# Rotation by a lane shuffle, three gate tiles moved ahead, and latent-attention scores for two heads at a time, in a two-layer encoder trunk

## The chip, the cores and the metric

The kernel runs on one core of one Trainium2 chip. The metric is the device time of one execution in microseconds (us), as the median of several executions. The engines are named as in the profile: PE (TensorE, matrix products), DVE (VectorE), ACT (ScalarE), POOL (GpSimd) and SP (SyncE, which issues the loads). Each engine works through its own list of instructions in a fixed order, and semaphores tie the lists together: an instruction whose input isn't ready holds up all that stands behind it on its engine.

## The reference

256 tokens of width 2048 pass through two layers; all numbers are fp32. What bears on the change is the first half of a layer:

```python
z = rmsnorm(x, g_mix[i]) @ w_in[i]
dq, dk, dv, cq, ckv, kr, ga, gb = split(z)      # 1024, 1024, 1024, 512, 256, 64, 2048, 2048 columns
# A: 8 heads, two softmax maps each (64 wide): weights = probs0 - lam * probs1; od = weights @ dv
qf = rmsnorm(cq) @ w_q_up                       # 8 heads of 128 + 64: q_nope, q_rope
kvf = rmsnorm(ckv) @ w_kv_up                    # 8 heads of 128 + 128: k_nope, v
k_rope = apply_rope(kr)                         # 64 wide, one for all heads
# B: scores = (q_nope @ k_nope + apply_rope(q_rope) @ k_rope) * scale; om = softmax(scores) @ v
m = sigmoid(ga) * (od_normed @ w_branch_diff) + sigmoid(gb) * (om @ w_branch_mla)
x = x + m @ w_out
```

`apply_rope` takes the halves x1 and x2 of the 64 columns and gives x1\*c - x2\*s and x2\*c + x1\*s: column d is combined with column d ± 32. Behind this come the SwiGLU feed-forward part and the gated embedding of the layer, which the change doesn't touch.

## The kernel before, in words

**Layout.** Tokens lie along the free axis (256), features along the 128 partitions. An activation tile is kept as two halves, `[hi | lo]`, 512 columns (`split`, L247: ACT writes hi, DVE the difference). A weight piece of 128x1024 is loaded by SP and split in the same way by ACT (`whi`, L187) and DVE (`wlo`, L187 too, recorded under L75): `piece`, L173. A product (`product`, L220; `pair`, L231, for two output tiles of a narrower weight) then runs for each 128x128 weight tile one matmul of 512 columns (hi times `[hi | lo]`, L212) and one of 256 columns (lo times hi, L216). The text calls these two a pair of matmuls. `joined` (L240) adds the two halves of the result: an ACT copy, `join`, and a DVE addition, `a`.

**Order of the first half of a layer.** The values of the differential attention come first, then the latents, then the loop over eight differential heads (`pipelined`, L650). For a head, `scores` (L398) makes two 128x256x2 maps by twelve 64-row matmuls (L406, maps in turn), `exps` (L409) takes the maxima (DVE, L412) and exponentials (ACT, L415), two blocks b per map; the weights are turned by PE (`turned`, L419 to L426: four transposes at L424, one ACT copy `wt`, L426), and `diff_out` (L626) multiplies them with the values (PE, L632), copies the result out (ACT, `fa`, L635) and sums its squares (ACT, L637). Between these steps, the generator `beside` (L573) hands out other products to fill PE: queries and keys of later heads, `keys_up`, the shared key through `narrow` and `rotated`, then `queries_up` for n = 8, 0, 2, 10 (8 and 10 are the rotated parts), `settle` (L639, transposes at L647), and last n = 4 and 6. Then come the latent values, and a second `pipelined` loop over eight latent heads (L678 to L692), filled with the sixteen tiles of the first gate. The sixteen tiles of the second gate and the merging loop follow.

**Rotation.** `rotated` (L363) uses PE: an fp32 matmul with a constant 128x128 matrix (`swap`, or `swaps` for the key, L367) exchanges columns d and d ± 32 of the tile; for the key another one (`halves`, L366) copies its 64 rows onto both halves of the partitions. DVE multiplies with the tables and adds. The shared key is written into two tiles, `krs[0]` with its lower 64 rows filled and `krs[1]` with its upper 64, the others zero. There are five rotations in a layer: the key and four query tiles, each of which holds two heads.

**Latent scores.** `mla_weights` (L670) makes a head's map by twelve matmuls over all 128 rows, each of 256 columns: for each of two blocks three for the plain part and three for the rotated part, where the tile of the other head is multiplied with the zeros of `krs`.

**What decides the order.** The program is written as above, and a scheduler then orders each engine's list by its own estimate of time. PSUM has four banks for products (`mm`), two for the maps (`S`) and two for small results (`at`); a matmul into a bank waits until the last reader of its previous contents is done. The split weight pieces have three buffers each, so ACT can split a fourth piece only when PE has finished with the first.

Of the kernel before, what the change touches and what calls it, by code (L numbers as in the profile page):

```python
# [12 lines left out]
F32 = mybir.dt.float32  # L13
# [6 lines left out]
P = 128  # L20
T = 256
# [18 lines left out]
BOTH = 6  # L40
PAD = 96 - 64 - 8
STEP = 48
NO_SYNC = mybir.DependencyInfo(mybir.DependencyClass.NoSync, mybir.DependencyReason.DATA)

TWO_PI = 2.0 * math.pi
# [8 lines left out]
def encoder(ctx, tc, x, p, positions, cols, lams, wq, wk, wv, wcq, wckv, wkr, wga, wgb,  # L54
# [16 lines left out]
    def bank(ps=ps_at, tag="at", name="at", shape=(P, 2 * T)):  # L71
        return ps.tile(list(shape), F32, tag=tag, name=name)

    def tt(o, a, b, op):
        return V.tensor_tensor(out=o, in0=a, in1=b, op=op)  # L75
# [171 lines left out]
    def split(u, src, gain=None):  # L247
        hi, lo = u[:, :T], u[:, T:]
        if gain is None:
            return A.activation(hi, src, AF.Copy), tt(lo, src, hi.bitcast(F32), ALU.subtract)  # L250
        return A.activation(hi, src, AF.Copy, scale=gain), stt(lo, src, gain, hi.bitcast(F32), ALU.mult, ALU.subtract)
# [104 lines left out]

    krs = [const.tile([P, 2 * T], F32R, name=f"kr{j}") for j in range(2)]
    for t in krs:  # L360
        nc.gpsimd.memset(t.bitcast(F32), 0.0)

    def rotated(a, c_, s_, o=None):  # L363
        r = bank()
        if o is None:
            PE.matmul(r[:, T:], halves, a, start=True, stop=True)  # L366
        PE.matmul(r[:, :T], swap if o is not None else swaps, a, start=True, stop=True)  # L367
# [117 lines left out]
    for L in range(DEPTH):  # L485
# [87 lines left out]
        def beside():  # L573

            for h in range(2, DH):
                if h < 6:
                    keys_up(2 * h - 4)
                elif h == 7:
                    rotated(joined(narrow(wkr[L], ua)), crm, srm)
                yield  # L580
                queries_keys(h)
                yield
            settle(0)
            for n in (8, 0, 2, 10):
                queries_up(n)
                yield
            settle(4)
            for n in (4, 6):
                queries_up(n)

        def gate(w, store, n):
            tt(store(n), joined(product(w[L, n], ua)), R, ALU.mult)

        def gate_a(n):
            if n % 2 == 0:
                gas.append(fa(n // 2))
            return gas[n // 2][:, n % 2, :]
# [6 lines left out]
        gas, gbs = [], []  # L604

        def sigmoid(sg):
            si = A.activation(sg, sg, AF.Sigmoid)
# [57 lines left out]


        oms = ub[8:]
        todo = iter(range(NC))
# [24 lines left out]


        for n in range(NC):
            gate(wgb, gate_b, n)
        ms = ua
        for n in range(NC):
            ga, gb = (t[n // 2][:, n % 2, :] for t in (gas, gbs))
# [186 lines left out]
        ("g_q_latent0", 4), ("g_q_latent1", 4), ("g_kv_latent0", 2), ("g_kv_latent1", 2), ("g_subln", 2)]  # L886


def rope_constants():


    c = np.zeros((P, 4 + 3 * P), np.float32)
    f32 = np.float32
    for base, dim in ((0, 16), (2, 64)):
        inv = f32(THETA) ** (-np.arange(0, dim, 2, dtype=f32) / f32(dim))
        for q in range(P):
            d = q % 64
            if d < dim:
                c[q, base] = inv[d % (dim // 2)]
                c[q, base + 1] = -1.0 if d < dim // 2 else 1.0  # L900
    for q in range(P):
        c[q, 4 + (q ^ 32)] = 1.0
        for m in (q, q ^ 64):
            c[q, 4 + P + (m ^ 32)] = 1.0
            c[q, 4 + 2 * P + m] = 1.0
    return c


# [18 lines left out]
def laid_out(a):  # L927
    a = {k: np.asarray(v) for k, v in a.items()}
    w_in = a["w_in"]
    cut = np.cumsum([0, 1024, 1024, 1024, QR, KVR, 64, DM, DM])  # L930
    z = [w_in[:, :, cut[j] : cut[j + 1]] for j in range(8)]
    up = a["w_q_up"].reshape(DEPTH, QR, MH, 192)
    kv = a["w_kv_up"].reshape(DEPTH, KVR, MH, 256)
    flat = lambda w: w.reshape(w.shape[0], w.shape[1], -1)
    named = {f"{n}{i}": a[n][i] for n in ("g_mix", "g_ffn", "g_ple", "g_q_latent", "g_kv_latent") for i in range(DEPTH)}
    named["g_final"] = a["g_final"]
    named["g_subln"] = a["g_subln"]
    return {
        "x": np.ascontiguousarray(a["x"][0].T.reshape(NC, P, T).transpose(1, 0, 2)),
        "p": np.ascontiguousarray(a["p"][:, 0].transpose(0, 2, 1).reshape(DEPTH, 2, P, T).transpose(0, 2, 1, 3)),  # L940
        "positions": np.ascontiguousarray(a["positions"]),
        "cols": np.ascontiguousarray(np.concatenate([columns(named[n]) for n, _ in COLS], axis=1)),
        "lams": np.ascontiguousarray(np.stack([a["lambda_q1"], a["lambda_q2"], a["lambda_k1"], a["lambda_k2"]], axis=1).reshape(1, -1)),
        "wq": tiles(z[0]), "wk": tiles(z[1]), "wv": wide(z[2]), "wcq": tiles(z[3]), "wckv": tiles(z[4]),
        "wkr": np.ascontiguousarray(z[5].reshape(DEPTH, NC, P, 64).transpose(0, 2, 1, 3)).reshape(DEPTH, P, NC * 64), "wga": tiles(z[6]), "wgb": tiles(z[7]),
        "w_q_up": tiles(np.concatenate([flat(up[..., :128]), flat(up[..., 128:])], axis=2)),
        "w_kn": tiles(flat(kv[..., :128])), "w_v": wide(flat(kv[..., 128:])),
        "w_bd": tiles(a["w_branch_diff"]), "w_bm": tiles(a["w_branch_mla"]), "w_out": tiles(a["w_out"]),
        "w_gate": tiles(a["w_gate_up"][:, :, :DFF]), "w_up": tiles(a["w_gate_up"][:, :, DFF:]),
        "w_down": tiles(a["w_down"]), "w_pin": tiles(a["w_ple_in"]), "w_pg": tiles(a["w_ple_gate"]),  # L950
        "rope_c": rope_constants(),
    }
# [17 lines left out]
```

## Time and profile before

| | |
|---|---|
| median of 3 executions | 2838.24 us (2837.36 to 2838.51) |
| the profiled execution | 2838.84 us, of which the span that the records cover is 2837.0 us |
| granted PE clock, mean | 0.999 of full |
| PE busy | 2826.8 us (100%), 16743 instructions |
| DVE busy | 2073.0 us (73%), 3537 instructions |
| ACT busy | 1527.5 us (54%), 2548 instructions |
| DMA | 531.49 MB, mean 187 GB/s |

A row of the timeline has the start of an instruction in us from the start of the span, its duration, its engine, the line in the kernel, and what it writes and reads. Matmuls are pipelined, so the start of the next instruction, not the duration, tells what one costs. In square brackets stands the time that the engine was idle before it, and what ended that. "x12" is a run of twelve alike. An fp32 matmul with fp32 operands leaves two records.

### The profile page before, as it was taken

How to read it: one execution, taken by the hardware profiler on the slowest of the kernel's cores; microseconds unless marked ns; L12 is line 12 of the kernel's file. 1: busy time of each engine (PE TensorE's matmuls, PEld its weight loads, DVE VectorE, ACT ScalarE, POOL GpSimd, SP SyncE). 2: the span in 40 equal slices, each digit the busy share in tenths (PEclk: the TensorE clock that was granted, in tenths of full speed). 3: DMA queues.
4: the chain of work that ended last, by engine and by line, in shares of the span. 5: the costliest groups of instructions: out<-in, count | busy, mean ns of one | idle time of the engine just before them, and what ended most of it. 6: DMA issues, size and time to landing. Idle time of an engine off the chain costs nothing.

```text
span 2837.0 us, 44038 instructions
## 1 busy us (share of the span) xinstructions
PE 2826.8 (100%) x16743; PEld 2498.5 (88%) x16743; DVE 2073.0 (73%) x3537; ACT 1527.5 (54%) x2548; POOL 1.9 (0%) x15
## 2 busy tenths in 40 slices
PE   9999999999999999999999999999999999999998
PEld 7888888888888888888888888888888888888888
DVE  7997658776666766677869976687766666666777
ACT  6676545554444444455646755555544444444556
POOL 0000000000000000000000000000000000000000
PEclk9999999999999999999999999999999999999999
DMA  7544466666665566566665445666666656666664
GB/s 244 169 161 149 162 194 197 192 194 193 187 199 193 182 198 201 194 193 194 193 192 169 155 150 168 195 197 194 193 193 187 199 193 187 202 194 194 193 193 155
DMA packets 156596, 531.49 MB, mean 187 GB/s; under 512 B 16992, under 2 KB 24160, under 8 KB 156384
## 3 DMA queue, kind: packets, MB, share of 16 engines
q1 hardware_dynamic: 155952, 528.09, 58.9%
q8 instruction: 131, 2.15, 0.3%
q14 instruction: 81, 0.66, 0.1%
q10 hardware_dynamic: 432, 0.59, 0.1%
HBM read 526.52 MB, written 2.10 MB: 186 GB/s over the span
## 4 chain that ended last, share of the span: by engine, by line
PE 99%; DMA 1%; DVE 0%; ACT 0%; issue 0%; SPq 0%; DVEq 0%; ACTq 0%
PE mm L212 61%; PE mm L216 31%; PE S L406 1%; PE mmv L462 1%; PE mmv L460 1%; PE mmv L461 1%; DMA w<-in_wv 1%; PE at L424 1%; PE at L632 1%; PE at L689 0%; PE mm L776 0%; PE mm L392 0%; DVE wlo L75 0%; PE at L647 0%; DVE a L75 0%; PE at L367 0%
## 5 line engine op out<-in xcount | busy, mean ns | idle before, releaser
L187 ACT ACTIVATE whi<-w 128x1024 fp32r<-128x1024 f32 (+2 forms) x1030 | 1063.1, 1033 | 1241.4 <-issue 704.3
L75 DVE TENSOR_TENSOR wlo<-w,whi 128x1024 fp32r<-128x1024 f32 (+2 forms) x1030 | 1224.4, 1189 | 676.5 <-ACT whi L187 667.8
L212 PE MATMUL mm<-ub,whi 128*128 128x512 f32 x3936 | 1342.3, 390 | 0.3
L212 PE MATMUL mm<-ua,whi 128*128 128x512 f32 x3712 | 1271.4, 390 | 0.0
L216 PE MATMUL mm<-ub,wlo 128*128 128x256 f32 x3936 | 1085.1, 276 | 0.0
L216 PE MATMUL mm<-ua,wlo 128*128 128x256 f32 x3712 | 1027.3, 277 | 0.0
L212 PEld LDWEIGHTS mm<-ub,whi 128*128 128x128 f32 x3936 | 738.2, 188 | 153.1 <-DVE a L75 0.7
L212 PEld LDWEIGHTS mm<-ua,whi 128*128 128x128 f32 x3712 | 696.0, 188 | 142.0
L216 PEld LDWEIGHTS mm<-ub,wlo 128*128 128x128 f32 x3936 | 738.8, 188 | 1.1
L216 PEld LDWEIGHTS mm<-ua,wlo 128*128 128x128 f32 x3712 | 696.9, 188 | 2.4 <-DVE wlo L75 0.6
L75 DVE TENSOR_TENSOR a<-mm,join 128x256 f32<-128x256 f32 (+1 forms) x423 | 175.1, 416 | 1.6 <-ACT join L805 1.4
L242 ACT ACTIVATE join<-mm 128x256 f32<-128x256 f32 x452 | 166.5, 370 | 5.2 <-PE mm L216 4.8
L75 DVE TENSOR_TENSOR xT<-xT,mm 128x256 f32<-128x256 f32 x256 | 106.8, 420 | 41.5 <-PE mm L216 37.7
L75 DVE TENSOR_TENSOR a<-a,row 128x256 f32<-128x256 f32 (+1 forms) x209 | 87.5, 422 | 5.9
L75 DVE TENSOR_TENSOR a<-a 128x256 f32<-128x256 f32 x120 | 50.8, 425 | 4.0
L460 PE MATMUL mmv<-whi,ua 128*128 128x512 f32 x128 | 50.1, 395 | 1.7 <-ACT whi L187 1.7
L75 DVE TENSOR_TENSOR ua<-a,ua 128x256 fp32r<-128x256 f32 x120 | 49.9, 417 | 1.0 <-ACT ua L250 1.0
L461 PE MATMUL mmv<-whi,ua 128*128 128x512 f32 x128 | 49.6, 391 | 0.0
L250 ACT ACTIVATE ua<-a 128x256 fp32r<-128x256 f32 x120 | 48.2, 403 | 2.6 <-DVE a L75 2.6
L415 ACT ACTIVATE E<-S,nm 128x256 f32<-128x256 f32 x96 | 44.2, 472 | 2.1 <-DVE nm L81 2.0
L462 PE MATMUL mmv<-wlo,ua 128*128 128x512 f32 x128 | 43.8, 393 | 0.1
L75 DVE TENSOR_TENSOR ssq<-ssq,sq 128x256 f32<-128x256 f32 x96 | 40.1, 417 | 0.3 <-ACT sq L280 0.3
(195 smaller groups left out, 1209.8 us busy)
## 6 DMA issues: line engine op xcount, KB each, us to landing
w<-in_w_gate SPq DMA_DIRECT2D x176, 512.0 KB, 4.7
w<-in_w_up SPq DMA_DIRECT2D x176, 512.0 KB, 4.7
w<-in_w_down SPq DMA_DIRECT2D x128, 512.0 KB, 4.1
w<-in_wga SPq DMA_DIRECT2D x64, 512.0 KB, 3.8
w<-in_wgb SPq DMA_DIRECT2D x64, 512.0 KB, 4.1
w<-in_w_out SPq DMA_DIRECT2D x64, 512.0 KB, 4.6
w<-in_w_pg SPq DMA_DIRECT2D x64, 512.0 KB, 4.7
w<-in_w_down SPq DMA_DIRECT2D x64, 384.0 KB, 3.7
```

Source lines behind the costliest of these rows:

```text
L75: return V.tensor_tensor(out=o, in0=a, in1=b, op=op)
L187: last_split[:] = A.activation(hi[:, :m], w[:, :m], AF.Copy), tt(lo[:, :m], w[:, :m], hi[:, :m].bitcast(F32), ALU.subtract)
L212: lead = PE.matmul(acc, hi[:, s], u, start=start, stop=False)
L216: rest = PE.matmul(acc[:, T:], lo[:, s], u[:, :T], start=False, stop=stop)
L242: A.activation(t, acc[:, T:], AF.Copy)
L250: return A.activation(hi, src, AF.Copy), tt(lo, src, hi.bitcast(F32), ALU.subtract)
L406: PE.matmul(S[:, b, :], q[:, b * P : (b + 1) * P], k, start=j == 0, stop=j == len(pairs) - 1)
L415: last_exp[0] = A.activation(E[:, b, :], S[:, b, :], AF.Exp, bias=nm[:, b : b + 1], scale=scale, accum_out=sm[:, b : b + 1])
L424: PE.transpose(tp[:, kb, b * P : (b + 1) * P], W[:, b, kb * P : (kb + 1) * P], ident)
L460: PE.matmul(banks[half][b], xh, hi[:, s], start=a + j == 0, stop=False)
L461: PE.matmul(banks[half][b], xl, hi[:, s], start=False, stop=False)
L462: last_mm[:] = [PE.matmul(banks[half][b], xh, lo[:, s], start=False, stop=a + j == n - 1)]
```

## The change

1. **Shuffle.** `rotated` exchanges the columns on DVE with `stream_shuffle`, which permutes within groups of 32 partitions. For that, the 64 rotated columns of the weights are put into another order on the host (`LATENT_ORDER`: partners 16 apart), and the tables with them. The matmul at L367 is gone; the key's matmul at L366 stays. The key is one tile, `kr`, whose two halves of 64 rows both hold the key.
2. **Early gates.** Three tiles of the first gate are computed inside `beside`, around `queries_up(4)` and `queries_up(6)`, and kept in tiles of their own.
3. **Two heads at a time.** `mla_weights` works on a pair of heads with both banks `S`: first twelve plain matmuls, then twelve matmuls on 64 rows each, in turn on rows 0 to 63 (first head) and 64 to 127 (second head). Each is chained behind the one before (`issue_after`), which sets PE's order and adds no wait. The loop over latent heads is written out anew; the filling is the rest of the first gate and then tiles of the second.

```diff
-    swap, swaps, halves = (rc[:, 4 + j * P : 4 + (j + 1) * P] for j in range(3))
+    halves = rc[:, 4 : 4 + P]
...
-        u = stat.tile([P, 2 * T], F32R, tag="sums", name="sums", bufs=1)
+        u = operand(tmp.tile([P, 2, T], F32R, tag="vs", name="sums", bufs=2))
...
-    krs = [const.tile([P, 2 * T], F32R, name=f"kr{j}") for j in range(2)]
-    for t in krs:
-        nc.gpsimd.memset(t.bitcast(F32), 0.0)
+    kr = const.tile([P, 2 * T], F32R, name="kr")
     def rotated(a, c_, s_, o=None):
-        r = bank()
         if o is None:
-            PE.matmul(r[:, T:], halves, a, start=True, stop=True)
-        PE.matmul(r[:, :T], swap if o is not None else swaps, a, start=True, stop=True)
+            r = bank()[:, :T]
+            PE.matmul(r, halves, a, start=True, stop=True)
+        else:
+            r = a
         t = scratch("sh", 2)
-        tt(t, r[:, :T], s_, ALU.mult)
-        tt(a, a if o is not None else r[:, T:], c_, ALU.mult)
+        V.stream_shuffle(t, r, SWAP16)
+        tt(t, t, s_, ALU.mult)
+        tt(a, r, c_, ALU.mult)
         tt(a, a, t, ALU.add)
         if o is None:
-            for j, t in enumerate(krs):
-                split(t[64 * j : 64 * j + 64], a[64 * j : 64 * j + 64])
+            split(kr, a)
...
+    SWAP16 = [(j + 16) % 32 for j in range(32)]
...
             settle(4)
             for n in (4, 6):
+                gate(wga, gate_a, next(todo))
                 queries_up(n)
+            gate(wga, gate_a, next(todo))
...
+        todo = iter(range(2 * NC))
+        def fill_gate():
+            n = next(todo)
+            gate(*((wga, gate_a, n) if n < NC else (wgb, gate_b, n - NC)))
...
-        def mla_weights(h):
-            E = weights()
-            S, = scores(three(qn[h], kn[h]) + three(qr[h // 2], krs[h % 2]))
-            r = exps(S, E, MLA_SCALE)
+        def mla_weights(m):
+            hs = 2 * m, 2 * m + 1
+            Ss = [bank(ps_s, "S", "S", (P, 2, T)) for _ in hs]
+            terms = [(S, b, q, k) for S, h in zip(Ss, hs) for b in range(2) for q, k in three(qn[h], kn[h])]
+            rows = slice(0, 64), slice(64, P)
             for b in range(2):
-                ts(E[:, b, :], E[:, b, :], r[:, b : b + 1], None, ALU.mult)
-            return E
+                for pairs in zip(*(three(qr[m][r], kr[r]) for r in rows)):
+                    terms += [(S, b, q, k) for S, (q, k) in zip(Ss, pairs)]
+            done = []
+            for i, (S, b, q, k) in enumerate(terms):
+                with ExitStack() as stack:
+                    if done:
+                        stack.enter_context(tc.issue_after(done[-1].ins))
+                    done.append(PE.matmul(S[:, b, :], q[:, b * P : (b + 1) * P], k, start=i in (0, 6), stop=i > 21))
...
-            vs = weights("E1", F32R)
+            vs = weights("vs", F32R)
...
-        pipelined(mla_weights, mla_out, MH, lambda: gate(wga, gate_a, next(todo)))
-        for n in range(NC):
-            gate(wgb, gate_b, n)
+        nxt = mla_weights(0)
+        for m in range(MH // 2):
+            Ws = nxt
+            fill_gate()
+            nxt = mla_weights(m + 1) if m + 1 < MH // 2 else None
+            for k, W in enumerate(Ws):
+                if k:
+                    fill_gate()
+                out_ = mla_out(2 * m + k, W)
+                next(out_)
+                fill_gate()
+                next(out_, None)
+        for n in todo:
+            gate(wgb, gate_b, n - NC)
...
+LATENT_ORDER = [q // 32 * 16 + q % 16 + q % 32 // 16 * 32 for q in range(64)]
```

The scheduler orders the changed program anew. Up to the end of the loop over differential heads the lists are nearly the same; the places that differ and matter here are three. All are from layer 0; at these places layer 1 has the same rows, apart from the numbers of tiles and one cut that the last paragraph names. Lines of the changed kernel are numbered a little higher: its L213 and L217 are the product's two matmuls, L188 is `whi`, L251 the hi half of `split`, L647 `diff_out`'s matmuls, L650 and L652 its copy and squares, L662 the transposes of `settle` and L696 the latent scores.

First, PE around the end of the differential loop, before the change: the last pair of matmuls of `queries_up(2)`, then the first plain scores of latent heads 0 and 1 around the four transposes of head 6 (they read E), then the first of the four pairs of half of the next `queries_up`, which take turns with the rows at `ub_100` to `ub_103`.

```order
L212 MATMUL mm<-ub_103,whi 128x512
L216 MATMUL mm<-ub_103,wlo 128x256
L406 MATMUL S<-fb_1291,fa_2579 128x256 x3
L424 MATMUL at<-ident,E 128x128 x4
L406 MATMUL S<-fb_1303,fa_2595 128x256 x3
L212 MATMUL mm<-ub_100,whi 128x512
L216 MATMUL mm<-ub_100,wlo 128x256
```

Three more such pairs and two rotated-score matmuls follow there, and only then head 6's L632 MATMUL at<-vals,wt. The same place after the change: the eight pairs of `queries_up(10)` end, and then stand the transposes of head 6, its multiplication with the values (it reads wt, ACT's copy of the transposes), six plain scores of latent head 0, and the first pairs of the first early gate tile.

```order
L217 MATMUL mm<-ub_103,wlo 128x256
L424 MATMUL at<-ident,E 128x128 x4
L647 MATMUL at<-vals,wt 128x128 x4
L696 MATMUL S<-fb_1288,fa_2572 128x256 x6
L213 MATMUL mm<-ua_76,whi 128x512
L217 MATMUL mm<-ua_76,wlo 128x256
```

What moved: no product stands any more between the transposes and the multiplication that needs them, nor between that and the scores.

Second, ACT at the same place after the change. E and E_2514 are the exponentials of differential head 7, wt, fa_2600 and ssd belong to head 6, ub_107 is a rotated query tile (second half of `queries_up(8)`), whi is the weight piece of `queries_up(4)`.

```order
L188 ACTIVATE whi<-w_2799 128x1024
L426 ACTIVATE wt<-at 128x512
L650 ACTIVATE fa_2600<-at 128x256
L652 ACTIVATE fa_2600,ssd<-fa_2600 128x128
L251 ACTIVATE ub_107<-a 128x256
L415 ACTIVATE E,sm<-S,nm 128x256 x2
L652 ACTIVATE fa_2600,ssd<-fa_2600 128x128
L415 ACTIVATE E_2514,sm<-S,nm 128x256 x2
```

Before the change the same exponentials stood ahead of that head's copies:

```order
L415 ACTIVATE E,sm<-S,nm 128x256 x2
L415 ACTIVATE E_2521,sm<-S,nm 128x256 x2
L250 ACTIVATE fa_2642<-a 128x256
L242 ACTIVATE join<-mm 128x256
L187 ACTIVATE whi<-w_2858 128x1024
L250 ACTIVATE ub_106<-a 128x256
L426 ACTIVATE wt<-at 128x512
```

What moved: the four exponentials of head 7 went from ahead of head 6's `wt` to behind its output copy `fa`, the first square and a split.

Third, PE in the latent loop after the change, at the second pair of heads (the third and fourth are alike): within a gate's product stand the plain scores of head 2, of head 3, and the twelve matmuls on 64 rows, without anything between.

```order
L213 MATMUL mm<-ua_83,whi 128x512
L696 MATMUL S<-fb_1483,fa_2619 128x256 x6
L696 MATMUL S<-fb_1495,fa_2635 128x256 x6
L696 MATMUL S<-kr,ub_107 128x256 x12
L424 MATMUL at<-ident,E 128x128 x4
L217 MATMUL mm<-ua_83,wlo 128x256
```

What moved: a head's twelve 128-row matmuls have become six, and twelve 64-row ones serve two heads. For the first pair of heads the twelve are cut by other work into seven and five (in layer 1, eight and four).

More of the change, by code (lines that the diff above doesn't have):

```diff
@@ L42 @@
 STEP = 48
+FIRST = 3
 NO_SYNC = mybir.DependencyInfo(mybir.DependencyClass.NoSync, mybir.DependencyReason.DATA)
@@ L594, in gate_a, with gate_tile @@
         def gate_a(n):
-            if n % 2 == 0:
+            if n < FIRST:
+                return gate_tile(n)
+            if n % 2 == 0 or n == FIRST:
                 gas.append(fa(n // 2))
-            return gas[n // 2][:, n % 2, :]
+            return gas[-1][:, n % 2, :]
+        def gate_tile(n):
+            if n == len(early):
+                early.append(stat.tile([P, T], F32, tag=f"early{n}", name=f"early{n}", bufs=1))
+            return early[n]
         def gate_b(n):
@@ L602, in gate_b @@
             return gbs[n // 2][:, n % 2, :]
-        gas, gbs = [], []
+        gas, gbs, early = [], [], []
+        todo = iter(range(2 * NC))
+        def fill_gate():
+            n = next(todo)
+            gate(*((wga, gate_a, n) if n < NC else (wgb, gate_b, n - NC)))
         def sigmoid(sg):
@@ L667, in encoder @@
         oms = ub[8:]
-        todo = iter(range(NC))
-        def mla_weights(h):
-            E = weights()
-            S, = scores(three(qn[h], kn[h]) + three(qr[h // 2], krs[h % 2]))
-            r = exps(S, E, MLA_SCALE)
-            for b in range(2):
-                ts(E[:, b, :], E[:, b, :], r[:, b : b + 1], None, ALU.mult)
-            return E
+        def mla_weights(m):
[3 more added lines that the diff above has]
+            rows = slice(0, 64), slice(64, P)
+            for b in range(2):
+                for pairs in zip(*(three(qr[m][r], kr[r]) for r in rows)):
[6 more added lines that the diff above has]
+                    done.append(PE.matmul(S[:, b, :], q[:, b * P : (b + 1) * P], k, start=i in (0, 6), stop=i > 21))
+            got = []
+            for S, tag in zip(Ss, ("E", "E1")):
+                E = weights(tag)
+                r = exps(S, E, MLA_SCALE)
+                for b in range(2):
+                    ts(E[:, b, :], E[:, b, :], r[:, b : b + 1], None, ALU.mult)
+                got.append(E)
+            return got
         def mla_out(h, W):
             v = head(vm, slice(None), h)
-            vs = weights("E1", F32R)
+            vs = weights("vs", F32R)
             vh, vl = vs[:, :, :P], vs[:, :, P:]
@@ L690, in mla_out @@
             split(oms[h], o[:, :T])
-        pipelined(mla_weights, mla_out, MH, lambda: gate(wga, gate_a, next(todo)))
-        for n in range(NC):
-            gate(wgb, gate_b, n)
+        nxt = mla_weights(0)
[12 more added lines that the diff above has]
+            gate(wgb, gate_b, n - NC)
         ms = ua
         for n in range(NC):
-            ga, gb = (t[n // 2][:, n % 2, :] for t in (gas, gbs))
+            ga = early[n] if n < FIRST else gas[n // 2 - FIRST // 2][:, n % 2, :]
+            gb = gbs[n // 2][:, n % 2, :]
             sigmoid(ga)
@@ L896, in rope_constants @@
         for q in range(P):
-            d = q % 64
+            d = q % 64 if dim < 64 else LATENT_ORDER[q % 64]
             if d < dim:
@@ L901, in rope_constants @@
     for q in range(P):
-        c[q, 4 + (q ^ 32)] = 1.0
         for m in (q, q ^ 64):
-            c[q, 4 + P + (m ^ 32)] = 1.0
-            c[q, 4 + 2 * P + m] = 1.0
+            c[q, 4 + m] = 1.0
     return c
```

6 lines of the change are left out of this document (3 added, 3 removed).

## The prediction

> **What bounds the kernel now.** I read the page's busy times first, then the shares of the chain that ended last, then PE's waits.
>
> ```profile
> PE 2826.8 (100%) x16743; PEld 2498.5 (88%) x16743; DVE 2073.0 (73%) x3537; ACT 1527.5 (54%) x2548; POOL 1.9 (0%) x15
> PE 99%; DMA 1%; DVE 0%; ACT 0%; issue 0%; SPq 0%; DVEq 0%; ACTq 0%
> PE mmv L460 <- ACT whi L187: 1.7, 1, 1.7
> PE at L476 <- DVE ones L115: 1.0, 1, 1.0
> ```
>
> PE is busy for 2826.8 of 2837.0 us, it holds 99% of the chain, and the waits that the trace names come to 2.7 us in the whole program. So the time is the sum of what PE issues plus the time PE stands still. Taking work off PE counts in full; taking it off another engine counts nothing; and making PE wait counts in full too. That third point decides here, because the change touches a stretch in which DVE has no time left:
>
> ```profile
> 200.00:212.00 12.00, 12.00 (x81) 10.49 (x80) 11.75 (x29) 10.97 (x33) 0.00 (x0) 1.00 0.50 171
> 212.00:222.00 10.00, 9.85 (x64) 8.78 (x63) 9.76 (x28) 8.98 (x27) 0.00 (x0) 1.00 0.40 131
> ```
>
> These two windows (length, then busy time of PE, weight loads, DVE, ACT, POOL, the granted clock, the DMA share) hold layer 0's `queries_up` and the end of the differential loop. DVE works for 11.75 of 12 and 9.76 of 10 us, ACT for 10.97 and 8.98. DMA is at 0.50 and 0.40, so weights are no limit.
>
> **Part 1, the shuffle: PE.** The rows are the group of swap matmuls, then PE's timeline around one of them.
>
> ```profile
> L367 PE MATMUL at<-a,rc 128*128 128x256 f32 x20 | 5.9, 379 | 0.0
> 214.86 0.28 PE L216 MATMUL mm<-ub,wlo 128*128 128x256 f32 x1
> 214.98 0.59 PE L367 MATMUL at<-a,rc 128*128 128x256 f32 x2
> ...
> 215.65 0.28 PE L216 MATMUL mm<-ub,wlo 128*128 128x256 f32 x1
> ...
> 216.12 0.39 PE L212 MATMUL mm<-ub,whi 128*128 128x512 f32 x1
> 216.34 0.28 PE L216 MATMUL mm<-ub,wlo 128*128 128x256 f32 x1
> 216.46 0.39 PE L212 MATMUL mm<-ub,whi 128*128 128x512 f32 x1
> ```
>
> Twenty records are ten swap matmuls, five in a layer. An undisturbed L212 has its L216 0.22 us later, and a pair takes 0.34. Here the L216 comes at 215.65, so the swap matmul that began at 214.98 cost 215.65 - 0.22 - 214.98 = 0.45 us; I take 0.43 to 0.45, and 10 x 0.44 = **-4.4 us**. The key's other matmul (L366) stays.
>
> **Part 1: DVE.** Each rotation gets a shuffle, and the key's two half splits become one, on ACT as well.
>
> ```profile
> L412 DVE TENSOR_REDUCE nm<-S 128x2 f32<-128x512 f32 x48 | 31.4, 681 | 1.6 <-PE S L406 1.6
> L524 DVE STREAM_SHUFFLE sh<-a 128x256 f32<-128x256 f32 x32 | 14.1, 441 | 0.0
> 214.47 0.41 DVE L75 TENSOR_TENSOR a<-mm,join 128x256 f32<-128x256 f32 x1
> 214.81 1.21 DVE L75 TENSOR_TENSOR wlo<-w,whi 128x1024 fp32r<-128x1024 f32 x1
> 215.94 0.47 DVE L78 SCALAR_TENSOR_TENSOR ub<-at,gsub,ub 128x256 fp32r<-128x256 f32 x1
> ```
>
> The shuffle of the same size that the kernel already has takes 0.44 us, some 0.1 less in a row of alike ones since starts overlap (an addition of 0.41 hands over after 0.34, a weight split of 1.21 after 1.13). Its mask is another one; that needn't cost, and if it did it would be DVE's time. Five shuffles a layer are 1.8 us of DVE, less 0.4 for the key. What hides them is PE's work; where DVE is full the cover is thin, and that is counted below with the wait.
>
> **Part 3: the scores.** First PE at a latent head before the change (twelve matmuls in groups of three, the last group and what follows), then at a differential head, which already has 64-row matmuls in turn on two halves of the rows.
>
> ```profile
> 277.55 0.52 PE L406 MATMUL S<-fb,fa 128*128 128x256 f32 x3
> ...
> 278.61 0.52 PE L406 MATMUL S<-kr,fc 128*128 128x256 f32 x3
> 278.98 0.60 PE L424 MATMUL at<-ident,E 128*128 128x128 f32 x4
> ```
>
> ```profile
> 177.76 0.28 PE L216 MATMUL mm<-ua,wlo 128*128 128x256 f32 x1
> 177.97 0.97 PE L406 MATMUL S<-fa,ub 64*128 64x256 f32 x12
> 178.87 0.65 PE L424 MATMUL at<-ident,E 128*128 128x128 f32 x4
> 179.28 0.48 PE L212 MATMUL mm<-ua,whi 128*128 128x512 f32 x1
> ```
>
> Twelve 128-row matmuls: 278.98 - 277.55 = 1.43 us, 0.12 each. Twelve 64-row ones: from 177.87, where the next 128-row matmul would have begun (0.11 after the L216), to 178.87, and the four transposes behind take 0.41 instead of 0.36 (a row below), so 1.05 us. For two heads, twelve rotated matmuls at 1.43 become a block at 1.05: -0.38 for each of eight pairs of heads, -3.0. The first pair's block of each layer is cut in two, so PE enters and leaves the 64-row form once more: at least the 0.10 + 0.05 seen here, at most the whole excess over six overlapped steps, which is some 0.35; I take 0.25, twice +0.25 = +0.5. Together **-2.5 us**, between -2.7 and, if the rows in turn did not overlap, +3.4 (the third rival). The chain of `issue_after` adds no semaphore between matmuls of one engine; its cost is its order.
>
> [...]
>
> **A stall that goes.** PE at the first latent scores before the change:
>
> ```profile
> 217.16 0.60 PE L424 MATMUL at<-ident,E 128*128 128x128 f32 x4
> 217.52 0.59 PE L406 MATMUL S<-fb,fa 128*128 128x256 f32 x3
> 218.26 0.50 PE L212 MATMUL mm<-ub,whi 128*128 128x512 f32 x1
> 218.59 0.28 PE L216 MATMUL mm<-ub,wlo 128*128 128x256 f32 x1
> ```
>
> Three scores should be done after 0.36, at 217.88; the L212 works from 218.59 - 0.22 = 218.37 on. PE stood 0.49 us, for the `whi` below, which is ready at 218.38. After the change that piece is needed only after an early gate's 5.5 us of pairs. What was late next is the wait that I count now. Twice, **-1.0 us**.
>
> **The waits that come.** In the new order PE has the four transposes of head 6, then at once its multiplication with the values, then at once six scores into a bank that still holds differential head 7. What releases each is on ACT. Its rows, and the chain's row for one head's multiplication with the values:
>
> ```profile
> 214.92 0.48 ACT L415 ACTIVATE E<-S,nm 128x256 f32<-128x256 f32 x1
> ...
> 215.82 0.49 ACT L415 ACTIVATE E<-S,nm 128x256 f32<-128x256 f32 x1
> ...
> 217.29 1.09 ACT L187 ACTIVATE whi<-w 128x1024 fp32r<-128x1024 f32 x1
> 218.24 0.45 ACT L250 ACTIVATE ub<-a 128x256 fp32r<-128x256 f32 x1
> 218.54 0.63 ACT L426 ACTIVATE wt<-at 128x512 f32<-128x512 f32 x1
> ...
> 221.09 0.39 ACT L635 ACTIVATE fa<-at 128x256 f32<-128x256 f32 x1
> 221.50 0.31 ACT L637 ACTIVATE fa<-fa 128x128 f32<-128x128 f32 x1
> ...
> 221.94 0.31 ACT L637 ACTIVATE fa<-fa 128x128 f32<-128x128 f32 x1
> ```
>
> ```profile
> 184.11 0.89 PE at L632 x8
> ```
>
> From start to start on ACT: whi 0.95, a split 0.30, fa 0.41, a square with its sum 0.44, an exponential with its sum 0.45 (0.90 for two). Let the transposes begin at 0; they end at 0.36. `whi` takes the buffer that the last L213 ahead of them frees: that began at -0.34 and lasts 0.39, so whi begins at 0.05, `wt` behind it at 1.00, and is ready at 1.62. **First wait: 1.62 - 0.36 = 1.26 us.** The multiplication lasts until 2.51. Then ACT: fa at 2.55, square 2.96, the split ub_107 3.40, head 7's first exponential 3.70, its second 4.15 to 4.63, which empties the bank. **Second wait: 4.63 - 2.51 = 2.12 us.** Behind PE's waiting scores stands the early gate, so nothing fills in. Together 3.4 us a layer, **+6.8 us** in two. The lower end is the first wait alone (2.5), if the second exponential isn't needed and starts overlap further it is some 5.5; the upper end depends on DVE.
>
> DVE must have ub_107's sum and head 7's maxima ready by 3.4. In its list from the weight split of `queries_up(2)` to the scaling of those maxima I count 37 instructions: four weight splits at 1.13, two maxima at 0.6 (0.68 less the overlap), four on single columns at an estimated 0.15, 27 others at 0.34 to 0.40: 15.9 us. PE meanwhile has 32 pairs at 0.34, a block of scores at 1.05 and three couples of transposes at half of the four's 0.36: 12.5 us. Both start from the same product's end, so DVE is done at about 3.3, just in time; each us that it is later adds a us per layer.
>
> **Part 2, the early gates:** the same pairs of matmuls at another place, no gain or loss of their own; their cover is in the wait above. Loads: SP issues the first gate's pieces ahead of `queries_up(4)` and (6); at a DMA share of 0.4 to 0.5 they come in time. In the later pairs of heads scores, transposes and outputs have gates between them, and I find no wait.
>
> **Sum:** -4.4 - 2.5 - 1.0 + 6.8 = -1.1 us. The profiled execution took 2838.84 (span 2837.0 and 1.8 around it), so 2837.7; it lies 0.6 above the median of the three executions, so on their scale **2837.1 us**.
>
> **The rivals.** A measurement of this kernel can tell about 0.2% (5.7 us) from no change, and by that the forecast is no change: chance 0.70.
>
> *The waits are not paid.* If ACT gets through its list early, the gain is 7.9 us: 2830.3, faster by 0.28%. For it speaks that PE shows no wait of this kind at all before. Against it: the order leaves nothing between, and the ACT durations are from rows. With half the waits paid the time would still be within 0.2%. Chance 0.17.
>
> *DVE decides the second wait.* The place is the maxima of head 7 behind three shuffles and four weight splits on a DVE that is 98% busy. It decides from the point where DVE is done more than 3.4 us after the transposes' start; to be slower than 2843.9 it must be 3.4 us later still, ten additions, in each layer. With 2 us it gives 2841. Chance of slower by this 0.05.
>
> *The rotated scores do not overlap,* since they begin with the lower rows where the differential heads begin with the upper ones: 12 x 0.12 + 0.35 = 1.79 instead of 1.05, 8 x 0.74 = +5.9, so 2843.0, and slower by over 0.2% with any other delay of 1 us. The differential heads' rows speak against it: there each head's matmuls take turns in the same way. Chance 0.08, counted as slower.
>
> *PE's clock falls in the new waits.*
>
> ```profile
> 23.72 0.50 PE L460 MATMUL mmv<-whi,ua 128*128 128x512 f32 x1 [1.68 <-ACT whi L187]
> 24.00:30.00 6.00, 5.94 (x26) 4.52 (x26) 4.44 (x7) 4.21 (x9) 0.00 (x0) 1.00 1.03 390
> ```
>
> After 1.68 us of waiting PE had the granted clock 1.00. 2.12 us is a little more, so I leave it out of the sum; at half the clock each us afterwards would lose half a us. This is within the forecast's 0.70, on its upper side.
>
> [...]
>
> **How the numbers follow.** Faster by over 0.2%: 0.17; within: 0.70; slower: 0.13. The range runs from just above the first rival (2831) to the third (2843), leaving out about a tenth at each end.
>
> **What would show it.** In PE's waits of the changed kernel: a row of the value matmul behind ACT's `wt`, twice about 1.3 us, and one of the latent scores behind ACT's E, twice about 2.1. If the second is over 2.5 with DVE named or busy, DVE decided. L696's 64-row blocks should last about 0.9 us a dozen; 1.4 means no overlap. PE's instructions should fall by 20 records of L367. The granted clock in the 10 us after the waits should be 1.00. The prediction is wrong if the waits are missing, or if PE waits in the later latent heads, where I found none.

## The result and the profile after

The changed kernel takes 2841.9 us (median of 22, 2839.51 to 2843.53); the kernel before took 2838.11 in 22 runs. The ratio is 1.0013 (95% interval 1.0007 to 1.0019): slower by 3.8 us where 1.1 us less was forecast. The time lies in the range, but the sign is wrong. The profiled execution took 2842.27 us, its span is 2840.5.

PE's waits in the changed kernel, the whole list (engine and what it ran, what it waited for, us, times, longest):

```profile
PE S L696 <- ACT E L415: 4.2, 2, 2.1
PE at L647 <- ACT wt L426: 2.2, 2, 1.1
PE at L477 <- DVE ones L116: 1.0, 1, 1.0
PE mmv L461 <- ACT whi L188: 0.3, 1, 0.3
```

The two forecast waits are there, once in each layer, behind the instructions that were named. PE's timeline of layer 0 from the transposes of differential head 6 on:

```profile
211.80 0.60 PE L424 MATMUL at<-ident,E 128*128 128x128 f32 x4
213.48 1.16 PE L647 MATMUL at<-vals,wt 128*128 128x128 f32 x8 [1.08 <-ACT wt L426]
216.76 1.65 PE L696 MATMUL S<-fb,fa 128*128 128x256 f32 x6 [2.12 <-ACT E L415]
218.21 0.63 PE L213 MATMUL mm<-ua,whi 128*128 128x512 f32 x1
218.63 0.41 PE L217 MATMUL mm<-ua,wlo 128*128 128x256 f32 x1
218.84 0.63 PE L213 MATMUL mm<-ua,whi 128*128 128x512 f32 x1
...
222.04 0.45 PE L213 MATMUL mm<-ua,whi 128*128 128x512 f32 x1
```

Counted from the end of the issue, PE stands from 211.80 + 0.36 = 212.16 to 213.48, 1.32 us, and again 2.1 to 2.4 us up to 216.76. Then comes what the sum lacked. Six scores take 218.21 - 216.76 = 1.45 us where six at 0.12 took 0.72, a pair of matmuls takes 0.64 instead of 0.34, and L213 lasts 0.63 instead of 0.39. At 222.04 it ends. The same in layer 1:

```profile
1624.24 1.16 PE L647 MATMUL at<-vals,wt 128*128 128x128 f32 x8 [1.08 <-ACT wt L426]
1627.52 0.98 PE L696 MATMUL S<-fb,fa 128*128 128x256 f32 x6 [2.12 <-ACT E L415]
1628.33 0.54 PE L213 MATMUL mm<-ua,whi 128*128 128x512 f32 x1
...
1628.88 0.63 PE L213 MATMUL mm<-ua,whi 128*128 128x512 f32 x1
...
1631.98 0.40 PE L213 MATMUL mm<-ua,whi 128*128 128x512 f32 x1
```

The windows give the reason; the third number from the right is the granted clock, the number behind the comma PE's busy time. They are cut at the changes of the clock (215.31, 222.13, 1628.43 and 1631.84) and otherwise 3.41 us from the next cut, which is the length of its fall in layer 1:

```profile
211.90:215.31 3.41, 1.66 (x13) 1.23 (x11) 3.41 (x10) 2.13 (x5) 0.00 (x0) 1.00 0.58 183
215.31:218.72 3.41, 1.96 (x8) 1.87 (x9) 3.27 (x12) 3.41 (x17) 0.00 (x0) 0.50 0.40 117
218.72:222.13 3.41, 3.41 (x13) 2.93 (x12) 3.41 (x12) 1.28 (x4) 0.00 (x0) 0.50 0.10 40
222.13:225.54 3.41, 3.41 (x22) 2.94 (x21) 2.46 (x5) 1.37 (x2) 0.00 (x0) 1.00 0.00 0
1625.02:1628.43 3.41, 1.29 (x11) 1.10 (x10) 3.41 (x12) 2.97 (x13) 0.00 (x0) 1.00 0.22 68
1628.43:1631.84 3.41, 3.41 (x12) 2.86 (x11) 3.27 (x11) 2.33 (x8) 0.00 (x0) 0.50 0.36 124
```

The granted clock is 0.50 from 215.31 to 222.13 in layer 0, of which PE works from 216.8 on, and from 1628.43 to 1631.84 in layer 1. In layer 0 that costs 1.45 - 0.72 = 0.7 us on the scores and 222.04 - 218.21 - 6 x 0.34 = 1.8 on six pairs; in layer 1 some 0.1 and 1631.98 - 1628.33 - 6 x 0.34 = 1.6. Together 4.2 us that no instruction and no wait accounts for (3.9 against the same instructions in the second run, below). The mean granted clock of an execution shows it, too: the fastest of the 22 (2839.51) has 0.999, the other 21 have 0.998.

To compare layers without the start of the program, I take the same instruction in both layers, the first transposes of the row of the latent norm (L325, in the changed kernel L326). Before, then after:

```profile
100.02 0.61 PE L325 MATMUL at<-ident,ry 128*128 128x128 f32 x4
1508.17 0.60 PE L325 MATMUL at<-ident,ry 128*128 128x128 f32 x4
```

```profile
99.11 0.61 PE L326 MATMUL at<-ident,ry 128*128 128x128 f32 x4
1509.86 0.61 PE L326 MATMUL at<-ident,ry 128*128 128x128 f32 x4
```

From the first to the second is one layer, 1408.15 us before and 1410.75 after: +2.60. From the second to the end of the span 1328.83 and 1330.64: +1.81. Below, such a pair of numbers is given for every run as "layer 0, layer 1 against before"; each is from one profiled execution.

### The profile page after: what moved, and what is told of

Same layout as the page of the kernel before. It is cut to its first block, busy times and chain, and to the rows that moved or that the text cites. A ratio compares the mean times of both kernels' runs of the same rounds, so it can differ in the third digit from the quotient of the medians.

```text
span 2840.5 us, 44006 instructions
## 1 busy us (share of the span) xinstructions
PE 2825.5 (99%) x16723; PEld 2493.4 (88%) x16723; DVE 2075.0 (73%) x3555; ACT 1526.1 (54%) x2546; POOL 1.0 (0%) x13
## 4 chain that ended last, share of the span: by engine, by line
PE 99%; DMA 0%; ACT 0%; DVE 0%; issue 0%; SPq 0%; DVEq 0%; ACTq 0%
PE mm L213 61%; PE mm L217 31%; PE mmv L463 1%; PE mmv L461 1%; PE mmv L462 1%; PE S L696 1%; PE at L424 1%; PE at L647 1%; PE S L406 1%; PE at L717 0%; DMA w<-in_wv 0%; PE mm L816 0%; PE mm L392 0%; ACT whi L188 0%; PE at L662 0%; DVE wlo L76 0%
## 5 line engine op out<-in xcount | busy, mean ns | idle before, releaser
L188 ACT ACTIVATE whi<-w 128x1024 fp32r<-128x1024 f32 (+2 forms) x1030 | 1063.3, 1032 | 1242.3 <-issue 709.0
L213 PE MATMUL mm<-ub,whi 128*128 128x512 f32 x3936 | 1341.3, 389 | 0.0
L213 PE MATMUL mm<-ua,whi 128*128 128x512 f32 x3712 | 1276.1, 391 | 0.0
L217 PE MATMUL mm<-ub,wlo 128*128 128x256 f32 x3936 | 1085.0, 276 | 0.0
L217 PE MATMUL mm<-ua,wlo 128*128 128x256 f32 x3712 | 1028.7, 278 | 0.0
L213 PEld LDWEIGHTS mm<-ub,whi 128*128 128x128 f32 x3936 | 738.3, 188 | 152.7
L213 PEld LDWEIGHTS mm<-ua,whi 128*128 128x128 f32 x3712 | 698.0, 188 | 143.4
L217 PEld LDWEIGHTS mm<-ub,wlo 128*128 128x128 f32 x3936 | 738.9, 188 | 0.9
L217 PEld LDWEIGHTS mm<-ua,wlo 128*128 128x128 f32 x3712 | 698.8, 188 | 1.6
L251 ACT ACTIVATE ua<-a 128x256 fp32r<-128x256 f32 x120 | 48.1, 403 | 2.6 <-DVE a L76 2.6
```

Source lines behind the costliest of these rows:

```text
L188: last_split[:] = A.activation(hi[:, :m], w[:, :m], AF.Copy), tt(lo[:, :m], w[:, :m], hi[:, :m].bitcast(F32), ALU.subtract)
L213: lead = PE.matmul(acc, hi[:, s], u, start=start, stop=False)
L217: rest = PE.matmul(acc[:, T:], lo[:, s], u[:, :T], start=False, stop=stop)
```

## The experiments

Theory W: the loss is the two waits of PE in each layer and the clock that falls in them; shuffle and scoring gain. Rivals: a part costs by itself (P), the early gates bring the waits (G), the clock falls for another reason (C), the mended order has a gain of its own (O). Each kernel was timed beside the kernel before on the same chip.

| run | median, before there | ratio (95%) | layer 0, layer 1 against before |
|---|---|---|---|
| the change | 2841.9, 2838.11 | 1.0013 (1.0007 to 1.0019) | +2.60, +1.81 |
| e1_order | 2832.12, 2838.72 | 0.9976 (0.9967 to 0.9986) | -3.29, -3.26 |
| e2_busy | 2837.95, 2838.72 | 0.9998 (0.9989 to 1.0006) | -0.36, -0.24 |
| e3_no_early | 2842.01, 2838.72 | 1.0011 (1.0003 to 1.0020) | +0.27, +1.72 |
| e4_order_no_early | 2836.64, 2838.72 | 0.9993 (0.9984 to 1.0002) | -0.94, -0.88 |
| e5_shuffle | 2837.38, 2838.50 | 0.9996 (0.9987 to 1.0004) | -0.49, -0.54 |
| e6_pairs | 2837.35, 2838.50 | 0.9994 (0.9986 to 1.0003) | -0.74, -0.68 |
| e7_early | 2839.49, 2838.50 | 1.0003 (0.9994 to 1.0012) | +0.37, +0.30 |
| e8_before_order | 2840.48, 2838.50 | 1.0007 (0.9999 to 1.0016) | +0.94, +1.03 |
| e9_settle | 2834.22, 2838.75 | 0.9983 (0.9975 to 0.9992) | -2.11, -2.03 |
| e10_upper | 2832.53, 2838.75 | 0.9979 (0.9970 to 0.9987) | -3.12, -3.02 |
| e11_one | 2831.57, 2838.75 | 0.9973 (0.9962 to 0.9983) | -3.67, -3.54 |

**Take the waits away, by the order alone.** The edit to the changed kernel, in `beside`:

```diff
-            for n in (8, 0, 2, 10):
+            for n in (0, 2, 8, 10):
```

> The whole change, with one edit: the products of queries_up come in the order 0, 2, 8, 10 instead of 8, 0, 2, 10. The instructions are the same, but in PE's list products now stand between the transposes of differential head 6, its multiplication with the values and the first latent scores. Theory W (the loss is the two waits of PE per layer and the clock that falls in them; all parts of the change gain): no PE wait over 0.5 us after the start, granted clock 1.00 throughout, and the gains alone remain: 4.4 for the swap matmuls, 2.2 to 2.6 for the scores, 1.0 for the old stall, 0.9 at the start, so 2829.5 to 2831 us. Rival P (a part costs by itself: the shuffles on a full DVE, or 64-row scores without a gain): the time stays at 2838 or above whatever the order.

Measured: 2832.12, 6.6 us below the kernel before. PE's waits in that run, the whole list, and two windows over the place:

```profile
PE at L477 <- DVE ones L116: 1.1, 1, 1.1
PE mmv L461 <- ACT whi L188: 0.8, 2, 0.5
```

```profile
214.00:218.00 4.00, 4.00 (x27) 3.63 (x27) 4.00 (x14) 3.72 (x12) 0.00 (x0) 1.00 0.60 208
218.00:222.00 4.00, 4.00 (x26) 3.58 (x25) 4.00 (x11) 3.77 (x11) 0.00 (x0) 1.00 0.46 157
```

Only the start's waits are left, PE is busy throughout and the clock is 1.00, while DVE is at 4.00 of 4.00. P falls: the same instructions in another order gain. The gain is 1 to 2 us smaller than expected: the layers give -6.55 where the terms made -7.6 to -8, and the 0.9 at the start isn't real (below).

**Keep the wait, but keep PE busy in it.** In `diff_out`, behind the multiplication with the values:

```diff
+            if h == 6:
+                for _ in range(5):
+                    PE.matmul(o[:, T:], ident, cos_m, start=True, stop=True)
             f = fa(h)
```

> The whole change in its own order, with five idle-time matmuls (identity times a table, fp32, 0.43 us each, into the unused half of the value result's bank, read by nobody) on PE behind head 6's multiplication with the values, in both layers: 2.2 us of work in a wait of 2.1 to 2.4. Theory W: the wait for E is nearly gone from PE's rows but no time is saved by that; the clock stays at 1.00, so the 4.3 us of slow matmuls go and the time is about 2837.6 (at most 2839 if the remaining wait of 1.1 now and then lowers the clock). Rival C (the clock falls for another reason, such as the kind or mix of instructions there): slow matmuls remain, 2841 to 2842.

Measured: 2837.95. PE's timeline and the windows of both layers:

```profile
213.80 1.16 PE L647 MATMUL at<-vals,wt 128*128 128x128 f32 x8 [1.08 <-ACT wt L426]
214.79 2.32 PE L650 MATMUL at<-cos_m,ident 128*128 128x256 f32 x10
216.77 1.07 PE L699 MATMUL S<-fb,fa 128*128 128x256 f32 x6
217.67 0.39 PE L213 MATMUL mm<-ua,whi 128*128 128x512 f32 x1
```

```profile
216.00:222.00 6.00, 6.00 (x38) 5.35 (x37) 6.00 (x22) 5.46 (x20) 0.00 (x0) 1.00 0.28 89
1624.00:1630.00 6.00, 6.00 (x38) 5.38 (x37) 6.00 (x22) 5.25 (x18) 0.00 (x0) 1.00 0.26 87
```

Little waiting was saved: from the transposes of head 6 (212.12 here, 211.80 in the changed kernel) to the scores it is 4.65 us instead of 4.96 (ACT's copy `fa` now stands behind the exponentials); in layer 1 it is 0.3 us less, too. The extra work is not needed by anything. Yet L213 lasts 0.39 at once and the clock is 1.00 in both layers. From the first score to the seventh L213 behind it takes 2.94 and 2.95 us, against 222.04 - 216.76 = 5.28 and 1631.98 - 1627.52 = 4.46 in the changed kernel: 2.3 and 1.5, together 3.9 us, are the price of the clock. The layers as a whole are shorter by 2.60 + 0.36 = 3.0 and 1.81 + 0.24 = 2.1 us, of which 0.3 each is the shorter wait. The same instructions ran at 0.50 in the changed kernel, where PE had stood still for 2.12 us ahead of them, and at 1.00 here, where it had worked, so their kind isn't what lowered the clock; C falls.

**Without the early gates.**

```diff
-FIRST = 3
+FIRST = 0
...
             for n in (4, 6):
-                gate(wga, gate_a, next(todo))
                 queries_up(n)
-            gate(wga, gate_a, next(todo))
```

> The change without the three early gate tiles (shuffle and scores by two heads only, order 8, 0, 2, 10). In its PE list the transposes, the multiplication with the values and six latent scores stand behind one another as with the whole change. Theory W in the form that shuffle and scoring together bring the waits: the same waits of 1.1 and 2.1 in each layer, slow clock after them, 2841 to 2842.5. Rival G (the early gates bring the waits): no such waits, 2830 to 2833.

Measured: 2842.01, and the same waits (4.2 and 2.2 in two). G falls. This run also shows something by accident. Layer 0's timeline, then the windows of layer 0 (two) and layer 1 (two):

```profile
213.61 1.16 PE L645 MATMUL at<-vals,wt 128*128 128x128 f32 x8 [1.08 <-ACT wt L426]
216.88 0.99 PE L694 MATMUL S<-fb,fa 128*128 128x256 f32 x6 [2.12 <-ACT E L415]
217.71 0.39 PE L213 MATMUL mm<-ub,whi 128*128 128x512 f32 x1
```

```profile
211.69:215.11 3.42, 2.00 (x15) 1.53 (x13) 3.42 (x10) 1.85 (x3) 0.00 (x0) 1.00 0.60 198
215.11:218.52 3.41, 1.64 (x11) 1.56 (x12) 3.27 (x11) 3.38 (x17) 0.00 (x0) 1.00 0.34 100
1621.40:1624.81 3.41, 1.16 (x8) 0.97 (x8) 3.41 (x10) 2.13 (x9) 0.00 (x0) 1.00 0.50 154
1624.81:1628.22 3.41, 2.92 (x11) 2.73 (x12) 3.27 (x13) 3.32 (x13) 0.00 (x0) 0.50 0.48 154
```

In layer 0 the same two waits left the clock at 1.00, and the layer is 0.27 us longer than before; in layer 1 the clock fell to 0.50, and it is 1.72 longer. So in this run the waits alone make a layer about as long as before, and the clock is the loss. Equal waits had both outcomes.

**The mended order without the early gates** (both edits above).

> Order 0, 2, 8, 10 as in the first run, without the early gate tiles. If the early gates are of no use once the order is mended, the time is that of the first run. If they are cover, what waits on ACT and DVE at the end of queries_up is no longer hidden: two waits of PE per layer at the latent values, of about 0.6 (for DVE) and 1.1 us (for ACT's copy of the values), 3.5 us in all, so 2833 to 2835.

Measured: 2836.64, a little above what was expected, with the waits that its order promised:

```profile
PE mmv L461 <- ACT whi L188: 2.3, 2, 1.3
PE mmv L461 <- ACT vals L468: 1.9, 2, 1.0
PE mmv L461 <- DVE a L76: 1.4, 2, 0.7
```

The first row is the program's start; the other two, 1.0 and 0.7 in each layer, stand at the latent values. The early gates are cover for these, worth 4.5 us in this order, of which 1.9 + 1.4 = 3.3 are these waits.

**The parts alone.** The shuffle alone is the kernel before with the change's `rotated`, column order and tables, but two key tiles and its old scores; the scoring alone is the change with the old `rotated`, `swap` matrices and column order and without early gates; the early gates alone are the kernel before with `gate_tile` and `fill_gate` (the tile `sums` moved to another tag for room).

> The kernel before with the shuffle alone (two zero-padded key tiles, scores one head at a time, no early gates). -4.4 us for the ten swap matmuls; some 0.9 at the start if the smaller table of constants is what shortened the wait there. By its order I expect PE to wait for DVE additions in the stretch of queries_up, 0.8 and 0.4 us and twice 0.2 per layer, some 3 us in two layers, of which 1.0 replaces the old stall. Theory W: 2835.5 to 2837, no wait over 1 us, clock 1.00. Rival P (shuffles too dear for DVE): above 2838.

> The kernel before with the scores of two heads at a time alone (swap matmuls and their three constant matrices kept, one key tile with both halves filled, no early gates). The rotated scores are 0.38 shorter for each of eight pairs of heads, some cuts cost 0.2 to 0.4 each, the old stall of 0.5 per layer is gone by the order: -2 to -3 us, 2835 to 2836, no wait over 0.5 us, clock 1.00. The wait at the start as before (1.7 us) if the table of constants sets it. If 64-row matmuls did not overlap in this order: 2842 or more.

> The kernel before with the three early gate tiles alone. No work less on PE; one short wait of 0.8 us per layer at the first product behind the latent loop by its order, in place of the old stall: no change to 1 us slower, 2838 to 2839.

Measured: 2837.38, 2837.35 and 2839.49. All three are slower than expected, by 0.4, 1.4 and 0.5 us, and the intervals of all three include no change. By the layers of the profiled executions, shuffle and scoring bring 1.0 and 1.4 us, and the early gates cost 0.7. In the run with the shuffle alone PE's waits begin with

```profile
PE mm L212 <- DVE a L75: 2.2, 6, 0.5
PE mmv L463 <- ACT whi L187: 1.7, 3, 0.8
```

so half of the 4.4 us that the swap matmuls took comes back as named waits for DVE's additions. In the run with the gates alone:

```profile
PE mm L217 <- DVE wlo L76: 1.5, 2, 0.8
```

that is the 0.8 us per layer at the first product behind the latent loop. The start tells that the smaller table of constants doesn't matter: with the large one the wait there was 1.7 (before) and 0.7 (scoring alone), with the small one 0.3 (the change) and 1.7 (shuffle alone). It varies from run to run, and I had been wrong to expect 0.9 us from it in the first run.

**The order alone, on the kernel before** (the first edit).

> The kernel before with the order 0, 2, 8, 10 alone. If the order as such were the gain of the first run, this would be faster too, by several us. Theory W: nothing to gain, the waits of the change aren't there; by its order two waits of 0.4 to 0.5 per layer: 2838 to 2840.

Measured: 2840.48, by the layers about 1 us slower in each; the interval just includes no change. There is no gain, so O falls as the cause of the first run's. This run's start holds the second accident, in the timeline, two windows and, last, the window of the kernel before at the same place:

```profile
24.08 0.51 PE L460 MATMUL mmv<-whi,ua 128*128 128x512 f32 x1 [1.66 <-ACT whi L187]
...
25.34 0.85 PE L462 MATMUL mmv<-wlo,ua 128*128 128x512 f32 x2
26.00 0.63 PE L460 MATMUL mmv<-whi,ua 128*128 128x512 f32 x1
```

```profile
22.38:25.80 3.42, 1.71 (x7) 1.09 (x7) 1.74 (x3) 2.78 (x4) 0.00 (x0) 1.00 0.93 299
25.80:29.21 3.41, 3.41 (x10) 2.62 (x9) 3.35 (x5) 2.42 (x6) 0.00 (x0) 0.50 1.04 400
22.26:25.67 3.41, 1.89 (x7) 1.27 (x8) 1.97 (x4) 3.02 (x5) 0.00 (x0) 1.00 0.92 299
```

It is the same instruction and the same wait, 1.66 us, as the row of 1.68 on which the prediction leaned. There the clock stayed at 1.00; here it fell to 0.50 at 25.80, 1.7 us after the wait had ended, and L460 takes 0.63 instead of 0.40.

**Another order without waits, rows begun from above, one early gate.** To the changed kernel: `settle(0)` moved behind `queries_up(2)`. To the first run's kernel: `rows = slice(64, P), slice(0, 64)`, by which each head of a pair gets the rotated scores of the other, so that part of the computation is changed while the work is the same; and `FIRST = 1` with one gate ahead of the loop over 4 and 6.

> The whole change with the order 8, 0, 2, 10 kept, and only the first settle moved from ahead of queries_up(8) to behind queries_up(2). Another way to the same end: by its PE list no wait of over 0.3 us. Theory W: what counts is that the waits are gone, not how, so about the time of the first run, 2832 to 2833, clock 1.00. Rival O (the order 0, 2, 8, 10 has a gain of its own): 2836 or more.

> The first run's kernel with the rotated scores in turns that begin on rows 64 to 127, as the differential heads do. If the turns overlap alike either way: no change, 2832 +- 0.5. If beginning below costs an overlap: 0.1 to 0.2 us for each of eight pairs of heads less, 2830.5 to 2831.5.

> The first run's kernel with one early gate tile instead of three. The fourth run (none) had 1.7 us of waits per layer at the latent values; by the PE list one tile is cover enough and one cut less of a block of 64-row scores remains: 2831.5 to 2832.5. If two or three tiles are needed as cover: up to 2835.

Measured: 2834.22, 2832.53 and 2831.57. None of the three has a wait of PE behind the start. The second way of taking the waits away gains 4.5 us, most of the first's 6.6, and lies between what W and O expected. Its first pair's twelve 64-row scores stand in four pieces (one, three, three and five) against three in the first run, some 0.5 us in two layers; the rest between them isn't explained here. Beginning on the upper rows changes nothing that could be told (2832.53 against 2832.12). One early gate (two pieces) does as well as three: 7.2 us below the kernel before, the fastest of all runs, though against the first run its interval overlaps.

## Why the prediction was wrong

**The two waits** were right in place, releaser and size: 1.26 and 2.12 us forecast, 1.08 and 2.12 named in the rows (1.32 and 2.4 by the issue, 0.3 us more in each layer than forecast). ACT did what was worked out:

```profile
211.88 1.06 ACT L188 ACTIVATE whi<-w 128x1024 fp32r<-128x1024 f32 x1 [0.80 <-PE mm L213]
212.85 0.58 ACT L426 ACTIVATE wt<-at 128x512 f32<-128x512 f32 x1
214.67 0.38 ACT L650 ACTIVATE fa<-at 128x256 f32<-128x256 f32 x1 [1.25 <-PE at L647]
```

From the transposes at 211.80, whi begins at +0.08 (0.05 forecast), wt at +1.05 (1.00), fa at +2.87 (2.55). DVE's maxima were in time, so the rival in which DVE decides did not come about.

**The swap matmuls** are gone, as forecast. **The scores** in the first pair of heads were cut in two and cost a little more than the 0.25 taken for a cut; the blocks of twelve behave as the differential heads' do (0.98 us against 0.97), and the rival of no overlap falls with the tenth run. With the waits and the clock out of the way, the layers gain 6.55 us (first run) where the terms made 7.9: too high by about a fifth. In that run the first pair's twelve stand in three pieces (two, six and four matmuls), not in the two that the sum allowed for; at 0.25 for a cut that is 0.5 of the missing 1.35.

**The step that failed** is the last rival: "After 1.68 us of waiting PE had the granted clock 1.00. 2.12 us is a little more, so I leave it out of the sum". One row was taken for a bound. What stood there was one outcome of something that went either way: after 1.66 us the clock fell to 0.50 in another run, and after two waits of 1.08 and 2.12 it was 1.00 in one layer of the third run and 0.50 in the other. In the profiled execution it cost 3.9 to 4.2 us. By the medians the run that keeps PE busy is 3.95 us faster than the change, 4.6 when each is taken against the kernel before beside it, and without its shorter waits (0.6) that is 3.3 to 4.0. Added to the forecast's -1.1, 3.3 to 4.2 gives +2.2 to +3.1; measured was +3.8. Two other terms erred the same way: the waits are longer by the issue, and the gains smaller.

**Why equal waits went either way** is not shown; the windows tell this much. Each time around such a wait the clock stayed at 0.50 for 3.41 us or for twice that: 215.31 to 222.13 and 1628.43 to 1631.84 in the changed kernel, 1624.81 to 1628.22 in the third run, 25.80 to 29.21 in the order alone. In the changed kernel the 1406.30 us from 222.13 to 1628.43 are 412 times 3.4133 us, and the 1204.90 us from 1631.84 to the fall behind the last matmul, at 2836.74, are 353 times the same. Where the clock didn't change, the windows are cut by counting such steps from the nearest change of that trace. The clock fell after steps in which PE was busy for 1.66, 1.29, 1.16 and 1.71 us, and at the end of the kernel before, at 2831.43, after one with 1.90. It stayed after steps with 2.00, 1.89 and 1.64 us:

```profile
2828.01:2831.43 3.42, 1.90 (x18) 1.66 (x16) 2.13 (x9) 3.38 (x8) 0.00 (x0) 1.00 0.41 153
2831.43:2834.84 3.41, 0.00 (x0) 0.00 (x0) 0.79 (x2) 0.71 (x2) 0.00 (x0) 0.50 0.94 376
```

So neither the length of one wait (1.66 us with a fall, 1.68 without) nor PE's busy time in a step sorts all of these cases.

That the parts don't add up was not forecast: shuffle alone, scoring alone and gates alone give -1.0, -1.4 and +0.7 over two layers, and all together +4.4 in one order and -6.55 in another. Here, where DVE is full (4.00 of 4.00 us), the order of the lists decided what a part was worth. Shuffle and scoring alone each got an order without the two waits; with both the scheduler put transposes, multiplication and scores behind one another, with or without the early gates. Why its estimate of time came out so was not tried.

## What to carry to other kernels

On a kernel whose matrix engine never waits, a wait can cost more than its length: here, after waits of 1.08 and 2.12 us, the clock was 0.50 for 3.41 us in one layer and 6.82 in the other, which cost another 1.5 and 2.3 us. Where the forecast has waits of this size, price that in, as a chance from 0 to its full cost, and don't take one row without the effect for a bound. When a change loses, look first for the place where its new order puts steps of one engine that each need another engine's result right behind one another; here, another order of four independent products turned +3.8 us into -6.6 with the same instructions, and idle work in the wait told the clock's share apart from the wait's.

## What the runs showed of the hardware

Waits of 1.08 and 2.12 us with 0.9 us of work between them were followed by a granted clock of 0.50 on PE in three of four cases looked at (both layers of the changed kernel, one of two in the third run), for 6.82 and 3.41 us in the changed kernel; a wait of 1.66 us was once, and one of 1.68 wasn't. The four changes of the clock around these waits in the changed kernel are 6.82, 1406.30 and 3.41 us apart, to 0.02 us 2, 412 and 1 times 3.4133. In the windows cut by that length the clock fell after 1.16 to 1.71 us of work on PE and, at the end of the kernel before, after 1.90; it stayed after 1.64, 1.89 and 2.00. With 2.32 us of matmuls whose result nobody reads in the place of the second wait, the clock was 1.00 in both layers. A shuffle of 128x256 has 0.44 us on DVE, and the load of its mask ahead of it 0.01:

```profile
217.51 0.01 DVE L369 LOAD_MASK_SELECT sh<-a  x1
217.51 0.44 DVE L369 STREAM_SHUFFLE sh<-a 128x256 f32<-128x256 f32 x1
```
